# Expert slot weights made group by group, the gather placed behind the activation's transposes, and modulation vectors closed in four groups of 256 columns

## The chip, the cores and the metric

The kernel runs on one core of one Trainium2 chip. A core has a matrix engine (TensorE, "PE" in the profile, with its weight loads shown apart as "PEld"), a vector engine (VectorE, "DVE"), an engine for activation functions (ScalarE, "ACT"), a general engine (GpSimd, "POOL") and a queue that issues transfers (SyncE, "SP"). Every engine works through its own list of instructions in order; semaphores join them. Weights lie in the chip's main memory and come by DMA into the on-chip memory (SBUF, 128 partitions); products go into PSUM, of which this kernel uses eight banks of 128 x 512 fp32. The metric is the device time of one execution in microseconds. Before the change the median of three runs is 2223.85 us (2223.41 to 2227.16).

## The reference

One input of 256 tokens x 1024 goes through two stacks of two layers each, all in fp32. The first stack has, per layer, a feed-forward block, a mixing block of three kinds of attention, a cross attention over 256 memory rows, and a second feed-forward block. The second stack is driven by a vector `c`: six modulation vectors per layer are made from it, and each layer has a mixer and a layer of 32 experts. Cut to what the change touches:

```python
c_act = silu(c)
for l in range(2):
    mod = c_act @ w_ada[l] + b_ada[l]                       # 6 vectors of 1024
    shift_m, scale_m, gate_m, shift_f, scale_f, gate_f = split(mod, 6)
    h = rms_norm(x, norm_mix[l]) * (1 + scale_m) + shift_m
    x = x + gate_m * mixer(h)
    h = rms_norm(x, norm_ffn[l]) * (1 + scale_f) + shift_f
    # a token takes 1 of 4 expert groups, and 2 of its 8 experts, with weights comb[token, expert]
    for each expert e:
        y += (silu(h @ w_gate[e]) * (h @ w_up[e]) * comb[:, e]) @ w_down[e]
    x = x + gate_f * y
```

The reference computes every expert for every token, most of them with weight 0. The kernel computes each expert only for the tokens that chose it.

## The kernel before, in words

**Modulation vectors.** They are not needed before the second stack, and are made during the first one, in the feed-forward blocks. `ada_step` (line 1320) gives for each of the 12 vectors (2 layers x 6) and each quarter of the 1024 rows of `w_ada` a small function per piece. DVE multiplies the piece by `c_act` and adds it into a tile `ada` of 128 x 1024 (lines 1357, 1359), so that what is left is a sum over the 128 partitions. With the fourth quarter, `rows` asks SP for the bias row and, for two of the six vectors, the gain of the norm, each broadcast to 32 partitions per half of 512 columns (lines 1329, 1332). Then `close` is put into a list of small tasks that are worked in between the dense products. It sums over the partitions with a product against ones, one product per half of 512 columns, each into its own strip of 32 PSUM partitions (line 1339, tile `adap`); DVE adds the bias and applies the gain (1342, 1344) on the strips, and SP writes one row of each strip into a table in memory, `mods` (1347). The second stack reads the vectors from there. Each fp32 product shows as two records on PE.

Around it, the first stack multiplies in a split form: each weight piece of 512 columns is split by ACT and DVE into a high and a low part (lines 288 to 293) into one of eight slots, and PE makes three products of it for each of the two halves of the tokens (`mm3`, lines 303 to 305). Raw weights come in transfers of 1 MB into four buffers, which SP issues as the buffers are freed (line 280).

**Rounds of experts.** `moe` (line 1833) first finds the chosen experts and the rank of each token among the tokens of an expert; each expert has 32 slots (`CAP`). `one_round` then works in eight groups q of four experts, 128 slots in all. For a group:
- `places` (1939) makes the 0/1 matrices `P[t]` (128 tokens x slots, one per half of the tokens),
- `gather(q)` (1951) multiplies the normed input by `P`, in two PSUM banks of four pieces each, and ACT and DVE evict the pieces in turn, with scale and shift, into `xg` (1956 on ACT for even pieces, 1958 on DVE for odd ones); `xg` has two buffers,
- `gate_up(q, k)` for k = 0 to 7 (1964) takes a 1 MB chunk of gate and up weights; the four experts stand on four strips of 32 columns of PE (tile `gu`),
- ACT makes silu of the gate half (2003), DVE multiplies by the slot weight and the up half (2004),
- two transposes of the activation and two of `P` (2007, 2009), copied by DVE and ACT (2013, 2014),
- four chunks of down weights (2021, tile `dn`), split into high and low by ACT and DVE, and the product with the transposed `P` that adds the slots back to their tokens (2026, tile `ymoe`).

The slot weights are `comb`, per token, brought into the order of the slots by a product with `P`: today for all eight groups at once, at k = 7 of the first group (line 1987, tile `comb`, 16 products of 4 columns), then a product with a mask and a sum on DVE (1990, 1992) into `cs`, of which line 2004 takes one column per group.

Each layer has 96 chunks of 1 MB (64 of gate and up, 32 of down); they go into a ring of buffers in the order of use, and SP issues a load when its buffer's chunk has been used (lines 1726, and 1723 for chunks that are loaded in two halves).

**What sets the order.** Where the code stands under `manual_schedule`, PE, ACT, DVE and POOL keep the order in which it is written. That holds for the first stack, the mixer, and the first part of a round: the loop over k of group 0, with the block of the slot weights. The loop over q behind it does not stand there: a planner orders it, by what is ready in its own model of time and, among that, by what is written earlier. SP's order is the planner's everywhere. PSUM has six banks of one pool (`ymoe` takes four for the whole round, the gather's banks and `dn` share two) and two of another (`tp`: `gu`, the transposes, the slot weights). Line 2044 and what follows repeat the round where an expert has more than 32 tokens; in the profile each layer has one round.

## Time and profile before

| | |
|---|---|
| median of three runs | 2223.85 us |
| profiled execution | 2221.21 us, with a span of 2219.2 us |
| PE busy | 2108.2 us, 95% |
| DVE busy | 1350.9 us, 61% |
| ACT busy | 1157.7 us, 52% |
| moved by DMA | 552.96 MB, mean 249 GB/s |
| first round of experts | about 1652 to 1852 us |
| second round | about 2005 to 2208 us |

All times are microseconds from the span's start. A row of the order of time has the start, the length, the engine, the line, the operation, what it writes and reads, and in brackets how long the engine sat idle before it and what ended that. Rows of one kind that follow each other are merged ("x32"). PE's records are pipelined and their ends are modelled: what a record costs in a stream is read from start to start. SP's rows are issues of transfers, not the transfers. A wait is put down to what came last.

### The profile page before, as it was taken

Reading aid. Unit: us, or ns where it says so; the run is one execution under the profiler, and the core shown is the slowest. Engines: PE = TensorE matmul, PEld = TensorE weight load, DVE = VectorE, ACT = ScalarE, POOL = GpSimd, SP = SyncE. Lnnn points to the kernel's source line nnn. Section 1 sums busy time; section 2 is a strip of 40 time slices with the busy share of each in tenths; the row PEclk is TensorE's granted clock in tenths of the full one; section 3 lists DMA queues with packets and bytes.
Section 4 is the critical chain, followed back from the end, with each engine's and each line's share of the span. In section 5 each row is a group of like instructions: output and inputs, shape, how many; then the busy total and the mean of one; then the engine's idle time right before and its main releaser. Section 6 shows DMA issues by size and latency. Waiting matters only on the chain. (4 is left out here: it accounts for less than half of the span.)

```text
span 2219.2 us, 28887 instructions
## 1 busy us (share of the span) xinstructions
PE 2108.2 (95%) x10668; PEld 1561.2 (70%) x10668; DVE 1350.9 (61%) x2472; ACT 1157.7 (52%) x2196; POOL 68.4 (3%) x76
## 2 busy tenths in 40 slices
PE   8999999999999999999999999998999887998895
PEld 7887878888788788777788878876765333775341
DVE  6876767765787687676677558766562114563111
ACT  6555677565655555466766556545842112762110
POOL 0000000000000000000000000002000001100000
PEclk9999999999999999999999999999999898999998
DMA  7875534553687577744356437766489998569998
GB/s 290 315 246 203 191 117 168 192 194 128 218 286 240 201 277 260 261 169 152 133 182 225 152 126 276 261 248 242 152 315 380 418 418 331 220 240 370 418 417 338
DMA packets 94551, 552.96 MB, mean 249 GB/s; under 512 B 11223, under 2 KB 12954, under 8 KB 41398
## 3 DMA queue, kind: packets, MB, share of 16 engines
q1 hardware_dynamic: 94398, 550.99, 67.0%
q8 instruction: 88, 1.44, 0.3%
q14 instruction: 65, 0.53, 0.1%
HBM read 549.85 MB, written 1.10 MB: 248 GB/s over the span
## 5 line engine op out<-in xcount | busy, mean ns | idle before, releaser
L289 DVE SCALAR_TENSOR_TENSOR hl<-raw,g_pre,hl 128x512 fp32r<-128x512 f32 (+1 forms) x296 | 214.2, 744 | 46.1 <-ACT hl L288 45.6
L288 ACT ACTIVATE hl<-raw,g_pre 128x512 fp32r<-128x512 f32 (+1 forms) x296 | 204.5, 719 | 62.4 <-PE gu L305 24.9
L289 DVE SCALAR_TENSOR_TENSOR pair<-raw,g_pre,pair 128x512 fp32r<-128x512 f32 (+1 forms) x296 | 207.6, 744 | 46.1 <-ACT pair L288 43.5
L293 DVE TENSOR_TENSOR hl<-raw,hl 128x512 fp32r<-128x512 f32 (+1 forms) x286 | 192.7, 688 | 68.8 <-ACT hl L291 65.5
L288 ACT ACTIVATE pair<-raw,g_pre 128x512 fp32r<-128x512 f32 (+1 forms) x296 | 196.6, 715 | 71.8 <-PE gu L305 52.0
L291 ACT ACTIVATE hl<-raw 128x512 fp32r<-128x512 f32 (+1 forms) x290 | 176.9, 626 | 94.3 <-PE y L305 41.1
L1964 PE MATMUL gu<-raw,xg 128*32 128x512 f32 x1024 | 144.0, 633 | 25.2 <-DMA raw<-w_gu 23.0
L293 DVE TENSOR_TENSOR pair<-raw,pair 128x512 fp32r<-128x512 f32 (+1 forms) x184 | 119.8, 692 | 69.7 <-ACT pair L291 69.3
L291 ACT ACTIVATE pair<-raw 128x512 fp32r<-128x512 f32 (+1 forms) x188 | 107.4, 621 | 91.6 <-PE y L305 64.3
L303 PE MATMUL gu<-pair,hh 128*128 128x512 f32 x320 | 127.3, 398 | 0.0
L303 PE MATMUL gu<-hl,hh 128*128 128x512 f32 x320 | 126.3, 395 | 0.0
L305 PE MATMUL gu<-pair,hl 128*128 128x512 f32 x320 | 125.1, 391 | 0.0
L305 PE MATMUL gu<-hl 128*128 128x512 f32 x320 | 125.0, 391 | 0.0
L304 PE MATMUL gu<-pair,hh 128*128 128x512 f32 x320 | 124.8, 390 | 0.0
L304 PE MATMUL gu<-hl,hh 128*128 128x512 f32 x320 | 124.8, 390 | 0.0
L1359 DVE SCALAR_TENSOR_TENSOR ada<-raw,cact,ada 128x512 f32<-128x512 f32 x168 | 122.0, 745 | 0.0
L1964 PEld LDWEIGHTS gu<-raw,xg 128*32 128x32 f32 x1024 | 29.8, 112 | 107.2 <-DMA raw<-w_gu 52.9
L1951 PEld LDWEIGHTS gather<-P,u 128*128 128x128 f32 x512 | 69.0, 214 | 30.3 <-issue 21.3
L2021 PE MATMUL dn<-raw,aT 128*32 128x512 f32 x512 | 79.2, 623 | 10.2 <-DMA raw<-w_dn 3.0
L2004 DVE SCALAR_TENSOR_TENSOR sil<-sil,cs,gu 128x256 f32<-128x256 f32 x16 | 7.7, 481 | 124.0 <-ACT sil L2003 123.7
L298 DVE TENSOR_TENSOR y<-dn,y 128x512 fp32r<-128x512 f32 x32 | 22.1, 692 | 98.5 <-ACT y L297 98.4
L1956 ACT ACTIVATE xg<-gather,fm 128x128 f32<-128x128 f32 x64 | 29.2, 457 | 95.4 <-PE gather L1951 80.6
(672 smaller groups left out, 4879.3 us busy)
## 6 DMA issues: line engine op xcount, KB each, us to landing
raw<-w SPq DMA_DIRECT2D x131, 1024.0 KB
raw<-w_gu SPq DMA_DIRECT2D x98, 1024.0 KB
raw<-win SPq DMA_DIRECT2D x71, 1024.0 KB
raw<-w_dn SPq DMA_DIRECT2D x54, 1024.0 KB
raw<-w_ada SPq DMA_DIRECT2D x48, 1024.0 KB
raw<-w_gu SPq DMA_DIRECT2D x60, 512.0 KB
raw<-w_out SPq DMA_DIRECT2D x16, 1024.0 KB
raw<-cross_wkv SPq DMA_DIRECT2D x16, 1024.0 KB
```

The lines of the kernel that those rows point to most:

```text
L288: nc.scalar.activation(hi, raw[:, c0:c0 + n], AF.Copy, scale=gain)
L289: nc.vector.scalar_tensor_tensor(lo, raw[:, c0:c0 + n], gain, hi.bitcast(F32), op0=ALU.mult, op1=ALU.subtract)
L291: nc.scalar.activation(hi, raw[:, c0:c0 + n], AF.Copy)
L293: eng.tensor_tensor(out=lo, in0=raw[:, c0:c0 + n], in1=hi.bitcast(F32), op=ALU.subtract)
L303: te.matmul(out, xh, wh, start=start, stop=False)
L304: te.matmul(out, xh, wl, start=False, stop=False)
L305: te.matmul(out, xl, wh, start=False, stop=stop)
L1359: nc.vector.scalar_tensor_tensor(self.ada[:, c], w, act, self.ada[:, c], op0=ALU.mult, op1=ALU.add)
L1951: te.matmul(ps[:, (k - k0) * 128:(k - k0 + 1) * 128], hm[t][:, k * 128:(k + 1) * 128], P[t][:, q * 128:(q + 1) * 128], start=(t == 0), sto ...
L1956: nc.scalar.activation(xg[:, k, :], v, AF.Identity, bias=sh, scale=g)
L1964: te.matmul(gu[32 * e:32 * e + 32, :], xg[:, k, 32 * e:32 * e + 32], w(e), start=(k == 0), stop=(k == 7))
L2021: te.matmul(dn[half][32 * e:32 * e + 32, :], aT[:, f, 32 * e:32 * e + 32], w(e), start=(f == 0), stop=(f == 1))
```

## The change

The change has two parts.

In `ada_step`, a vector is closed in four groups of 256 columns in place of two of 512: four products of 256 columns on four strips of 32 partitions, bias and gain broadcast in four pieces, DVE's operations on 128 x 256 in place of 64 x 512, and four rows written to `mods`.

In `one_round`, the slot weights of a group are made in the group itself, by two products of 4 columns into a tile of their own, with a product and a sum on DVE, written between the group's gate and up products and its activation. The block for all groups at once is gone. The gather of the next group is written behind the group's transposes and their copies, where it stood ahead of the activation. In the first gather of a round, piece k = 1 is evicted by ACT and not by DVE.

```diff
-            for g in range(2):
-                p, c0 = slice(32 * g, 32 * g + 32), g * 512
-                nc.sync.dma_start(bn[p, 0, :], self.a["b_ada"][l, i * D + c0:i * D + c0 + 512].unsqueeze(0)
-                                  .to_broadcast([32, 512]))
+            for g in range(4):
+                p, c0 = slice(32 * g, 32 * g + 32), g * 256
+                nc.sync.dma_start(bn[p, 0, 0:256], self.a["b_ada"][l, i * D + c0:i * D + c0 + 256].unsqueeze(0)
+                                  .to_broadcast([32, 256]))
                 if gain:
-                    nc.sync.dma_start(bn[p, 1, :], self.a[gain][l, c0:c0 + 512].unsqueeze(0).to_broadcast([32, 512]))
+                    nc.sync.dma_start(bn[p, 1, 0:256], self.a[gain][l, c0:c0 + 256].unsqueeze(0).to_broadcast([32, 256]))
...
-            for g in range(2):
-                nc.tensor.matmul(tp[32 * g:32 * g + 32, :], self.ones[:, 0:32], acc[:, g * 512:(g + 1) * 512],
+            for g in range(4):
+                nc.tensor.matmul(tp[32 * g:32 * g + 32, 0:256], self.ones[:, 0:32], acc[:, g * 256:(g + 1) * 256],
                                  start=True, stop=True)
-            row = fp.tile([64, 512], F32, tag="row", name="row")
-            nc.vector.tensor_add(row, tp[0:64, :], bn[0:64, 0, :])
+            row = fp.tile([128, 256], F32, tag="row", name="row")
+            nc.vector.tensor_add(row, tp[:, 0:256], bn[:, 0, 0:256])
             if gain:
-                nc.vector.scalar_tensor_tensor(row, row, 1.0, bn[0:64, 1, :], op0=ALU.add, op1=ALU.mult)
-            for g in range(2):
-                c0 = i * D + g * 512
-                nc.sync.dma_start(self.mod_dram[l:l + 1, c0:c0 + 512], row[32 * g:32 * g + 1, :])
+                nc.vector.scalar_tensor_tensor(row, row, 1.0, bn[:, 1, 0:256], op0=ALU.add, op1=ALU.mult)
+            for g in range(4):
+                c0 = i * D + g * 256
+                nc.sync.dma_start(self.mod_dram[l:l + 1, c0:c0 + 256], row[32 * g:32 * g + 1, :])
...
-                            if k % 2 == 0:
+                            if k % 2 == 0 or (first and k == 1):
                                 nc.scalar.activation(xg[:, k, :], v, AF.Identity, bias=sh, scale=g)
...
-                    xg = gather(0, {0: ((0, 1), (1, 2)), 1: ((2, 4),), 3: ((4, 8),)}[0])
+                    xg = gather(0, {0: ((0, 1), (1, 2)), 1: ((2, 4),), 3: ((4, 8),)}[0], first=True)
...
-                        if k == 7:
-                            comb_tp = self.tp("comb")
-                            for i in range(8):
-                                for t in range(2):
-                                    te.matmul(comb_tp[:, i * 4:(i + 1) * 4], P[t][:, i * 128:(i + 1) * 128],
-                                              comb[:, t, i * 4:(i + 1) * 4], start=(t == 0), stop=(t == 1))
-                            cw, cs = r2.tile([128, 8, 4], F32, name="cw"), r2.tile([128, 8], F32, name="cs")
-                            ve.tensor_mul(cw, comb_tp[:, 0:32].rearrange("p (q e) -> p q e", q=8),
-                                          self.misc[:, 34:38].unsqueeze(1).to_broadcast([128, 8, 4]))
-                            ve.reduce_sum(cs, cw, AX.X)
...
-                    if q < 7:
-                        xg = gather(q + 1)
+                    ctp, cw, cs = self.tp("comb"), r2.tile([128, 4], F32, name="cw"), r2.tile([128, 1], F32, name="cs")
+                    for t in range(2):
+                        te.matmul(ctp[:, 0:4], P[t][:, q * 128:(q + 1) * 128], comb[:, t, q * 4:(q + 1) * 4],
+                                  start=(t == 0), stop=(t == 1))
+                    ve.tensor_mul(cw, ctp[:, 0:4], self.misc[:, 34:38])
+                    ve.reduce_sum(cs, cw, AX.X)
...
-                    ve.scalar_tensor_tensor(sil, sil, cs[:, q:q + 1], gu[:, 256:512], op0=ALU.mult, op1=ALU.mult)
+                    ve.scalar_tensor_tensor(sil, sil, cs, gu[:, 256:512], op0=ALU.mult, op1=ALU.mult)
...
                     nc.scalar.activation(PT, tp[:, 256:512].rearrange("p (f s) -> p f s", f=2), AF.Copy)
+                    if q < 7:
+                        xg = gather(q + 1)
```

More of the change, by code (lines that the diff above doesn't have):

```diff
@@ L1942, in places, with gather @@
                                          op=ALU.is_equal)
-                def gather(q, cuts=((0, 4), (4, 8)), xg=None):
+                def gather(q, cuts=((0, 4), (4, 8)), xg=None, first=False):
                     if xg is None:
```

## The prediction

> **What bounds the kernel now.** I read the page first, then busy time by stage, then the order of time at the two places that the diff touches.
>
> ```profile
> span 2219.2 us, 28887 instructions
> PE 2108.2 (95%) x10668; PEld 1561.2 (70%) x10668; DVE 1350.9 (61%) x2472; ACT 1157.7 (52%) x2196; POOL 68.4 (3%) x76
> 30.00:1500.00 1470.00, 1455.96 (x6819) 1178.76 (x6818) 1062.83 (x1899) 876.59 (x1689) 27.44 (x40) 1.00 0.60 210
> 1692.00:1852.00 160.00, 136.97 (x869) 56.04 (x867) 26.17 (x53) 25.11 (x53) 0.00 (x0) 0.90 1.02 418
> 2045.00:2208.00 163.00, 133.53 (x861) 51.89 (x860) 26.49 (x54) 24.07 (x51) 0.00 (x0) 0.94 1.00 412
> ```
>
> The columns of the stretches are length, busy PE, PEld, DVE, ACT, POOL, granted clock, DMA share and GB/s. There are two regimes. In the first stack (to about 1500 us), where the modulation vectors are made, PE has work for all but 14 us of 1470 (clock 1.00), while DMA's share is 0.60. In the expert rounds (1652 to 1852 and 2005 to 2208) PE has gaps and DMA runs at share 1.00 to 1.02, some 412 to 418 GB/s. So an edit in the first stack is worth what it takes off PE's queue, and an edit in a round is worth only what it takes out of the DMA's idle time.
>
> **The closings of the modulation vectors.** One closing, PE's order of time (start, length, line):
>
> ```profile
> 75.16 0.39 PE L305 MATMUL gu<-hl 128*128 128x512 f32 x1
> 75.47 1.05 PE L1339 MATMUL adap<-ada,ones 128*32 128x512 f32 x4
> 76.46 0.50 PE L303 MATMUL gu<-pair,hh 128*128 128x512 f32 x1
> 1686.12 1.07 PE L1964 MATMUL gu<-raw,xg 128*32 128x512 f32 x8
> 1687.12 0.74 PE L2026 MATMUL ymoe<-y,PT 128*128 128x512 f32 x2
> 1971.08 1.07 PE go L1651 x24
> ```
>
> The closing's 4 records (two products of 512 columns, two records each) hold PE from 75.47 to 76.46, 0.99 us. The row of 1686.12 is one expert chunk: 8 records, four products of 512 columns on four column strips, from 1686.12 to 1687.12, 1.00 us. Twice the products in the same time: strips run side by side, and the time goes by columns. Five chunks back to back take 4.43 us (1662.21 to 1666.64, quoted below); with a lone one at 1.00 the other four take 0.86 each, so 0.14 of a lone chunk is its end draining. The four products of 256 columns are then 0.86/2 + 0.14 = 0.57 us, a gain of 0.43 us. Bounds: if each record had a slot of its own in PE's queue of the size that a chunk's 8 records show (0.86/8), 8 short records would take as long as before, a gain of 0. Against that stands the last row: 24 records of small products in 1.07 us, 0.045 us each, so 8 need only 0.36, less than the 0.43 of streaming. I take 0.43. There are 12 closings:
>
> ```profile
> L1339 PE MATMUL adap<-ada,ones x48: 592/604/618, 75.5 to 1493.4; 128*32 128x512 f32 x48
> L1342 DVE TENSOR_TENSOR row<-adap,bn x12: 671/681/684, 78.1 to 1494.0; 64x512 f32<-64x512 f32 x12
> L2013 DVE COPY aT<-actT 128x256 f32<-128x256 f32 x8 | 3.4, 421 | 4.2 <-PE actT L2009 4.2
> L1329 SPq DMA_DIRECT2D bn<-b_ada x24: 413/423/610, 62.3 to 1441.6; - x24
> L1332 SPq DMA_DIRECT2D bn<-n_mix x4: 413/427/733, 108.8 to 859.0; - x4
> L1332 SPq DMA_DIRECT2D bn<-n_ffn x4: 413/417/423, 662.5 to 1414.2; - x4
> L1347 SPq DMA_DIRECT2D mods<-row x24: 236/244/292, 78.8 to 1495.0; - x24
> ACT hl L288 <- DMA raw<-w: 21.9, 13, 3.4
> ACT pair L291 <- PE y L305: 64.3, 35, 3.3
> ```
>
> 48 records are 12 closings of 4, all between 75.5 and 1493.4 us, where PE is full: 12 x 0.43 = **5.2 us** (0 to 5.2). On DVE each row operation shrinks from 0.681 toward that of 128x256 elements (0.421 by the copy from PSUM), some 0.26 us; 12 of them and 4 of L1344 are about 4 us of DVE time, costed at nothing because PE's queue is what is full (DVE 1063 of 1470). SP gets dearer: L1329 and L1332 together go from 32 to 64 issues of about 0.42 us, L1347 from 24 to 48 of 0.244, so 32 x 0.42 + 24 x 0.244 = 19.3 us more of SP's time, 0.84 or 1.68 us ahead of a closing and 0.49 behind it. Weight loads queue behind these on SP, the splits (ACT L288/L291, DVE L289/L293) wait for the loads, and PE for the splits. I cost it at nothing: the splits more often stand waiting for PE to give a slot back (64.3 us in the one row, more in its fellows) than for a load (21.9 us in the other), so they run ahead by the slots there are, and a load that is 1 or 2 us late meets finished splits. Without that cover it is up to 19.3 us. The row also reaches the write to memory earlier, by 0.43 + 0.26 us, so SP stands less long at L1347.
>
> **The start of a round.** The first round's chain, then the second's:
>
> ```profile
> 1653.32 0.46 ACT L1956 ACTIVATE xg<-gather,fm 128x128 f32<-128x128 f32 x1 [4.73 <-PE gather L1951]
> 1653.79 1.28 ACT L1891 ACT_TABLE_LOAD   x1
> 1654.17 0.41 DVE L1958 TENSOR_SCALAR xg<-gather,fm 128x128 f32<-128x128 f32 x1 [2.03 <-PE gather L1951]
> 1654.50 2.50 DVE L1939 TENSOR_TENSOR P<-rank,misc 128x128 f32<-128x128 f32 x8
> 1659.24 1.06 PE L1964 MATMUL gu<-raw,xg 128*32 128x512 f32 x8 [0.73 <-ACT xg L1956]
> 1662.21 4.50 PE L1964 MATMUL gu<-raw,xg 128*32 128x512 f32 x40
> 1666.64 3.73 PE L1987 MATMUL comb<-comb,P 128*128 128x4 f32 x32
> 1670.24 5.45 PE L1951 MATMUL gather<-P,u 128*128 128x128 f32 x32
> 1677.02 0.63 PE L2021 MATMUL dn<-raw,aT 128*32 128x512 f32 x3
> ```
>
> ```profile
> 2012.54 1.07 PE L1964 MATMUL gu<-raw,xg 128*32 128x512 f32 x8 [1.52 <-ACT xg L1956]
> 2019.95 3.73 PE L1987 MATMUL comb<-comb,P 128*128 128x4 f32 x32
> 2023.54 3.82 PE L1951 MATMUL gather<-P,u 128*128 128x128 f32 x32
> 2028.70 0.63 PE L2021 MATMUL dn<-raw,aT 128*32 128x512 f32 x3
> ```
>
> Moving k = 1 of the first gather to ACT lets DVE begin the eight P pieces 1.9 us sooner: it now waits 2.03 us for the gather (1654.17) and only then goes on. ACT does 0.46 us more. Behind the P pieces DVE runs the weights' chain, whose second exponential stands on ACT ahead of the k = 2 eviction, for which PE waits at 1659.24 (0.73 us) and 2012.54 (1.52 us). ACT's table load for the exponential now comes behind the k = 1 eviction, so the chain gains about 1.2 us, not 1.9: PE gains **0.73 us** in the first round and **1.2** in the second (bounds 0 and the whole waits).
>
> **The slot weights.** Now 32 records of 4 columns stand between the last chunk of group 0 and the gather of group 1: 1666.64 to 1670.24, 3.60 us (3.59 in the second round), 0.1125 us a record. Behind them come the gather, the transposes and the first down products at 1677.02 and 2028.70. The change leaves 4 records there (0.45 us) and moves 28 to the other seven groups, one set of 4 in each: **3.15 us** leave this place in each round. The gather behind the transposes costs PE nothing of its own: it is ready while ACT and DVE make the activation, so I expect the planner to fill PE with gather records until the transposes are ready, and to put the rest behind them. From the end of group 0 to the first down product are now 10.4 us, in the second round 8.75, of which 3.59 are the sets, 3.82 the gather (5.45 in the first round) and the rest the transposes and the copy behind them. Without 3.15 of them they are 7.2 and 5.6; where the copy lies under gather records it is up to 1 us less. I use the 3.15, plus the start's 0.73 and 1.2: a shift of at least 3.9 and 4.3 us.
>
> What is late next? The moved sets cost 7 x 0.45 = 3.15 us of PE in groups 1 to 7, and two small DVE operations each; from 1692 and 2045 on DMA sets the pace and PE has gaps (137 of 160 us busy), so this lies in the gaps. Each new tile of the two-buffer PSUM pool is free again after the small DVE product, ahead of the transposes' tile, so the chunks of the next group don't wait for it.
>
> **What the shift is worth.** SP's issues and the DMA there:
>
> ```profile
> 1664.17 3.64 SPq L1723 DMA_DIRECT2D raw<-w_gu  x6
> 1678.89 6.64 SPq L1726 DMA_DIRECT2D raw<-w_gu  x5
> ```
>
> ```profile
> SPq L1726 <- PE dn L2021: 24.3, 6, 11.0
> ```
>
> ```profile
> 1676.00:1680.00 4.00, 4.00 (x36) 1.53 (x34) 1.15 (x3) 1.15 (x4) 0.00 (x0) 1.00 0.16 39
> 1680.00:1684.00 4.00, 4.00 (x20) 1.17 (x22) 0.69 (x1) 0.35 (x1) 0.00 (x0) 1.00 0.93 356
> 2028.00:2032.00 4.00, 4.00 (x34) 1.37 (x26) 1.05 (x3) 1.29 (x3) 0.00 (x0) 1.00 0.57 170
> 2032.00:2036.00 4.00, 4.00 (x23) 1.29 (x25) 0.69 (x1) 0.03 (x1) 0.00 (x0) 1.00 0.90 369
> ```
>
> From 1667.8 to 1678.89 SP issues nothing; it waits for the first down product to free a buffer (11.0 us, the longest). The transfers issued until then are over at about 1676, and DMA drops to 39 GB/s. Against 420 GB/s the two slices lose 4 x (381 + 64)/420 = 4.2 us in the first round, and 4 x (250 + 51)/420 = 2.9 us in the second. Shortfalls ahead of them I leave. The five loads behind the first hole are spread over 6.64 us, so the later ones wait for PE too; a shift of 3.9 us doesn't quite close a hole of 4.2: between 3.2 (the 3.15 alone) and 4.2 I take **3.7**. The second closes: **2.9**. Both are 0 if the issue doesn't move. Behind the holes DMA is full to the round's end, so its end, and all that follows, moves by this.
>
> One price works against spreading the sets. A chunk that is followed by work on the whole array takes 1.00 in place of 0.86 us, 0.14 for draining; with as much on the way back (an estimate) a set among chunks costs 0.45 + 0.28 = 0.73 us, seven of them 5.1 in place of 3.15. [...]
>
> **Sum.** 5.2 + 3.7 + 2.9 = 11.8 us less. The profiled execution took 2221.21 us, 2.0 around its span of 2219.2; it becomes 2209.4 with a span of 2207.4. The median of the runs, 2223.85, lies 2.6 above the profiled one; on it the forecast is **2212.0 us**.
>
> **The rivals.**
> *The closings gain nothing* (records are paced one by one, or the splits pace PE): -6.6, 2217.2. For it: DVE, whose splits feed PE, is the next fullest engine. Against: PE without a gap there, and the 0.045 us records.
> *The holes stay.* The planner's order is not written in the code; it may put group 1's chunks, or the whole gather with its evictions, ahead of the first down product, and the buffer that SP waits for comes as late as now. Only the closings count: -5.2, 2218.7. Against: the 3.15 us leave PE's queue whatever the order.
> *PE paces the rounds*, and each set pays both switches: per round 5.1 - 3.15 = 2.0 more less the start's 0.73 or 1.2, about +2 in all, so -5.2 + 2 = -3.2, 2220.7. For it: PE is full in the slices of the holes (4.00 of 4.00). Against: behind them DMA is full for 160 us while PE is not.
> *Slower: SP's queue.* The 32 broadcast issues and 24 writes stand in one queue with the weight loads. If loads become late by all of it, the closings' -5.2 turns into +14.1, and with the holes closed the sum is +7.5: 2231. It decides once 11.8 of the 19.3 us reach PE, that is where splits have under about 1 us of lead at most closings. For it: ACT waits 3.4 us for one load at worst. Against: 21.9 us of such waits in 13 places over 1500 us.
>
> **How the numbers follow.** Forecast 0.55; closings worthless 0.10; holes stay 0.17; PE paces 0.07; SP's queue 0.08; the last 0.03 for more than forecast: 4.2 in place of 3.7, the whole of the waits at the rounds' starts (0.73 + 1.52) and the slow gather of the first round mended (5.45 - 3.82 = 1.6) would be 4.4 more, 2207.6. The range from 2206 to 2222 holds all but the SP case and the tail of the others. No change can be told from 0.2%, 4.4 us: faster is below 2219.4, same to 2228.3. Faster: forecast, closings worthless, the better tail, and a little over half of the holes case, 0.78; same 0.14; slower 0.08.
>
> **What would show it.** Right: closings of 8 records that hold PE some 0.57 us; PE still without gaps before 1500; 4 comb records and not 32 behind group 0; SP's silence after the sixth half-load shorter by 4 us or more; no 4-us slice under 0.9 of DMA between there and the round's end; rounds shorter by 3.7 and 2.9 us, the mixing stage of the second layer unchanged. Wrong: PE gaps or ACT waits on weight loads around the closings; the first down product still 8 us behind group 0; DMA holes that only moved to a later group.

## The result, and the profile after

The changed kernel takes **2210.87 us** (median of 4 runs, 2210.41 to 2211.02), beside 2224.26 us (2223.41 to 2227.16, 4 runs) for the kernel before: ratio 0.9935, 95% interval 0.992 to 0.9951, 13.4 us less: a small gain, clear of the noise. The forecast was 2212.0. The profiled execution took 2211.02 us for a span of 2209.2; before they were 2221.21 and 2219.2, so between the two profiled executions there are only 10.2 us. Where the other 3 lie is part of what follows.

First the head of the page of the changed kernel, and busy time by the stretches that the prediction read (length, busy PE, PEld, DVE, ACT, POOL, granted clock, which is the share of full speed that PE was given, DMA share, GB/s):

```profile
span 2209.2 us, 29059 instructions
PE 2102.9 (95%) x10716; PEld 1559.4 (71%) x10716; DVE 1351.7 (61%) x2498; ACT 1159.1 (52%) x2198; POOL 68.3 (3%) x76
30.00:1500.00 1470.00, 1455.91 (x6886) 1181.98 (x6885) 1061.27 (x1903) 878.75 (x1694) 28.07 (x41) 1.00 0.60 210
1687.00:1847.00 160.00, 135.00 (x863) 54.23 (x855) 28.66 (x65) 22.98 (x48) 0.00 (x0) 0.91 1.02 417
2037.00:2198.00 161.00, 135.52 (x864) 53.00 (x860) 26.69 (x62) 22.14 (x48) 0.00 (x0) 0.90 1.00 412
```

The two regimes are as they were: PE is full to 1500 us (14 us of gaps in 1470, as before), and DMA is full in the rounds behind their first groups (1.02 and 1.00). The change did not alter what bounds a stage.

**A closing.** PE's order of time around the first closing of the changed kernel, then its groups and waits:

```profile
74.83 0.64 PE L1339 MATMUL adap<-ada,ones 128*32 128x256 f32 x8
75.40 0.50 PE L303 MATMUL gu<-pair,hh 128*128 128x512 f32 x1
...
L1339 PE MATMUL adap<-ada,ones x96: 379/391/403, 74.8 to 1488.0; 128*32 128x256 f32 x96
L1342 DVE TENSOR_TENSOR row<-adap,bn x12: 415/424/426, 77.4 to 1488.4; 128x256 f32<-128x256 f32 x12
L1329 SPq DMA_DIRECT2D bn<-b_ada x48: 320/420/1050, 61.6 to 1437.4; - x48
ACT hl L288 <- DMA raw<-w: 17.2, 9, 3.5
```

From 74.83 to 75.40 the 8 records hold PE for 0.57 us, where 4 held it for 0.99. SP's broadcasts doubled in number at the same 0.42 us each, and the row of ACT's waits for weight loads that the prediction read did not grow: 17.2 us in 9 places, before 21.9 in 13.

**Behind group 0 of the first round.** PE's order of time in the changed kernel, then what SP issued, its wait for the down products around the first round (1640 to 1700), and the 4-us slices there:

```profile
1660.65 0.61 PE L1992 MATMUL comb<-comb,P 128*128 128x4 f32 x4
1661.11 2.70 PE L1951 MATMUL gather<-P,u 128*128 128x128 f32 x22
1663.65 0.38 PE L2001 MATMUL actT<-ident,sil 128*128 128x128 f32 x2
1663.87 0.38 PE L2003 MATMUL actT<-ident,P 128*128 128x128 f32 x2
1664.09 1.28 PE L1951 MATMUL gather<-P,u 128*128 128x128 f32 x10
1665.30 1.92 PE L2017 MATMUL dn<-raw,aT 128*32 128x512 f32 x16
```

```profile
1658.17 3.39 SPq L1723 DMA_DIRECT2D raw<-w_gu  x6
1666.42 7.03 SPq L1726 DMA_DIRECT2D raw<-w_gu  x5
...
SPq L1726 <- PE dn L2017: 19.2, 8, 6.4
...
1660.00:1664.00 4.00, 4.00 (x38) 3.36 (x31) 1.12 (x4) 0.84 (x2) 0.00 (x0) 1.00 0.93 346
1664.00:1668.00 4.00, 4.00 (x32) 1.82 (x30) 1.73 (x6) 2.36 (x5) 0.00 (x0) 1.00 0.98 376
1668.00:1672.00 4.00, 4.00 (x23) 1.28 (x25) 0.61 (x1) 0.00 (x0) 0.00 (x0) 1.00 1.04 421
```

The planner filled PE as the prediction expected: one set of 4 slot-weight records, 22 gather records while ACT and DVE make the activation, the transposes, the last 10 gather records while DVE copies. The first down product stands 4.65 us behind the end of group 0 (1665.30 less 1660.65); before it was 10.38 (1677.02 less 1666.64). SP's silence behind the sixth half-load is 4.9 us (1661.56 to 1666.42) in place of 11.1, 6.2 shorter where 4 or more was forecast; in the second round it is 4.5 in place of 9.7. SP's longest wait for a down product in the first round is 6.4 us in place of 11.0, and the sum of these waits there 19.2 in place of 24.3. The slice of 39 GB/s is gone; the lowest share is 0.93, and from 1668 to the round's last issue no slice of 4 us is under 0.99. In the second round the lowest is 0.98, from 2012 to 2016.

**A ledger of the whole.** Two marks divide the time behind the first stack: the first product of the ranks (L1879, once a round) and SP's last issue of a down weight in each round. Each kernel was profiled twice (the second time as an experiment, below). The rank products, and the last issue of the first and the second round, of the kernel before; of its second profile; of the changed kernel; of its second profile:

```profile
L1879 PE MATMUL rank<-selb,beforeb x2: 206/207/208, 1651.0 to 2004.3; 128*128 128x32 bf16 x2
1842.80 0.33 SPq L1726 DMA_DIRECT2D raw<-w_dn  x1
2195.75 0.33 SPq L1726 DMA_DIRECT2D raw<-w_dn  x1
```

```profile
L1879 PE MATMUL rank<-selb,beforeb x2: 209/210/210, 1651.4 to 2007.2; 128*128 128x32 bf16 x2
1845.75 0.33 SPq L1726 DMA_DIRECT2D raw<-w_dn  x1
2197.57 0.33 SPq L1726 DMA_DIRECT2D raw<-w_dn  x1
```

```profile
L1879 PE MATMUL rank<-selb,beforeb x2: 206/206/207, 1645.8 to 1996.6; 128*128 128x32 bf16 x2
1834.49 0.33 SPq L1726 DMA_DIRECT2D raw<-w_dn  x1
2184.89 0.33 SPq L1726 DMA_DIRECT2D raw<-w_dn  x1
```

```profile
L1879 PE MATMUL rank<-selb,beforeb x2: 206/206/207, 1646.1 to 1997.8; 128*128 128x32 bf16 x2
1835.47 0.33 SPq L1726 DMA_DIRECT2D raw<-w_dn  x1
2185.87 0.33 SPq L1726 DMA_DIRECT2D raw<-w_dn  x1
```

| stretch | before, its second profile | changed, its second profile | difference of the means | predicted |
|---|---|---|---|---|
| start to first rank | 1651.0, 1651.4 | 1645.8, 1646.1 | -5.25 | -5.2 |
| first rank to last issue | 191.8, 194.35 | 188.7, 189.4 | -4.0 | -3.7 |
| to second rank (mixing stage) | 161.5, 161.45 | 162.1, 162.3 | +0.7 | 0 |
| second rank to last issue | 191.45, 190.4 | 188.3, 188.1 | -2.7 | -2.9 |
| to the end of the span | 23.45, 25.3 | 24.3, 23.5 | -0.5 | 0 |
| span | 2219.2, 2222.9 | 2209.2, 2209.4 | -11.75 | -11.8 |

Four profiles are few. Over all fourteen of this case the first rank starts at 1650.8 to 1652.2 us in the eight whose closings use two strips, and at 1645.8 to 1646.9 in the six with four, 5.0 less in the mean.

### The profile page after: what moved, and what is told of

The parts are those of the page before. It is cut to its first block, busy times and chain, and to the rows that moved or that the text cites. A ratio compares the mean times of both kernels' runs of the same rounds, so it can differ in the third digit from the quotient of the medians.

```text
span 2209.2 us, 29059 instructions
## 1 busy us (share of the span) xinstructions
PE 2102.9 (95%) x10716; PEld 1559.4 (71%) x10716; DVE 1351.7 (61%) x2498; ACT 1159.1 (52%) x2198; POOL 68.3 (3%) x76
## 3 DMA queue, kind: packets, MB, share of 16 engines
q8 instruction: 87, 1.43, 0.3%
## 5 line engine op out<-in xcount | busy, mean ns | idle before, releaser
L293 DVE TENSOR_TENSOR hl<-raw,hl 128x512 fp32r<-128x512 f32 (+1 forms) x286 | 191.8, 685 | 69.7 <-ACT hl L291 66.5
L1951 PE MATMUL gather<-P,u 128*128 128x128 f32 x512 | 76.0, 302 | 5.2 <-DVE xg L1958 3.8
L1997 ACT ACTIVATE sil<-gu 128x256 f32<-128x256 f32 x16 | 6.1, 384 | 137.0 <-PE gu L1964 137.0
```

The costliest lines, as they stand in the source:

```text
L293: eng.tensor_tensor(out=lo, in0=raw[:, c0:c0 + n], in1=hi.bitcast(F32), op=ALU.subtract)
L1951: te.matmul(ps[:, (k - k0) * 128:(k - k0 + 1) * 128], hm[t][:, k * 128:(k + 1) * 128], P[t][:, q * 128:(q + 1) * 128], start=(t == 0), sto ...
```

## The experiments

Each time stands beside runs of the kernel before on the same chip; a difference is one of medians, and brackets hold the 95% interval of the ratio.

### The two parts by themselves

closings_only is the kernel before with the changed rows() and close(). rounds_only is the changed kernel with these two put back. Of the two edits only the heads of the loops are shown:

```diff
 closings_only                      rounds_only
-for g in range(2):  # 512 columns  -for g in range(4):  # 256 columns
+for g in range(4):  # 256 columns  +for g in range(2):  # 512 columns
```

> The kernel before with the four-group closing alone. Theory A (PE paces the first stack and a closing costs its streamed columns): 12 x 0.43 = 5.2 us less, all of it before 1500 us, the two rounds as before, so that the rank products of the first and the second round both start 5.2 us sooner (1645.8, 1999.1) and the span is 2214.0. Rival B (a gain there is used up later, since the rounds wait for transfers): less than 3 us at the end. Rival C (the closing gains only together with the round's change): 0.

> The kernel before with the three edits of the expert rounds and the old closing. Theory A (the two parts add up): the rank products of the first round start as before (1651.0), those of the second 2.5 us sooner, the end 4.8 us sooner, span 2214.4. Rival B (the earlier end of the first stack changed what the rounds gain): the rounds' gain lies 1 us or more off 4.8.

Beside 2224.16 us: closings_only 2217.49 (2216.78 to 2218.74), ratio 0.9967 [0.9954, 0.9979], 6.7 less; rounds_only 2217.41 (2217.03 to 2217.67), 0.9963 [0.9949, 0.9977], 6.75 less. Together 13.4, all that the change gives: in the medians the parts add up. By the marks, the first rank starts at 1646.6 in closings_only and at 1651.1 in rounds_only, and the rounds are 192.1 and 190.6 us in the first, 187.8 and 188.4 in the second. So each part acts in its own stage. "The closings gain nothing" and "the holes stay" both fall.

The sizes do not fit as well as the sum. The first rank of closings_only is 4.4 us sooner than in the first profile of the kernel before, where 5.2 was expected, and its median gains 6.7; what the other 2 us are isn't shown. The rounds of rounds_only are 7.0 us shorter than in that profile, where 4.8 was expected. Both have a longer tail than it, 25.3 and 26.1 us in place of 23.45, so that their spans, 2216.3 and 2215.6, lie above the 2214.0 and 2214.4 that were expected.

### How a closing gets shorter

two_strips is the kernel before, with the same two strips of the array and the same row, but 4 products of 256 columns (8 records) in place of 2 of 512. broadcasts_x3 is the changed kernel with every broadcast of a bias or gain issued three times. Arguments left out are marked by dots:

```diff
 two_strips
-            for g in range(2):
-                matmul(tp[32 * g:32 * g + 32, :], ..., acc[:, g * 512:(g + 1) * 512], ...)
+            for h in range(2):
+                for g in range(2):
+                    c0 = g * 512 + h * 256
+                    matmul(tp[32 * g:32 * g + 32, h * 256:(h + 1) * 256], ..., acc[:, c0:c0 + 256], ...)
 broadcasts_x3
+                for _ in range(3):
                     nc.sync.dma_start(bn[p, 0, 0:256], ...)
                     if gain:
                         nc.sync.dma_start(bn[p, 1, 0:256], ...)
```

> The kernel before with each closing as four products of 256 columns, but on the two old strips, two products one behind the other on each: the same records as in the change (8 per closing), without the four strips. Transfers and DVE's operations as before. Theory A (strips run side by side, time goes by the columns of one strip): a closing holds PE 0.99 us as before, span 2219.2 within 1 us. Rival B (shorter products are cheaper by themselves): 0.57 us a closing, 5 us less. Rival C (records are paced one by one): 1.2 us a closing or more, 2 us longer.

> The changed kernel with each broadcast of a bias or gain row issued three times into the same place: 128 more issues on SP, some 54 us of its time in all, 3.4 or 6.7 us ahead of a closing. Theory A (splits run ahead of PE by up to eight slots, so late loads meet finished splits): under 1.5 us longer. Rival B (SP's queue is on the path once it is late by more than some 2 us): 10 us or more longer, with ACT waiting for weight loads around the closings.

Beside 2224.41 us: two_strips 2223.9 (2218.7 to 2232.06), 0.9999 [0.9987, 1.001]; broadcasts_x3 2210.38 (2209.77 to 2211.16), 0.9931 [0.9915, 0.9948]. The first closing on PE in two_strips:

```profile
75.90 1.06 PE L1341 MATMUL adap<-ada,ones 128*32 128x256 f32 x8
76.89 0.50 PE L303 MATMUL gu<-pair,hh 128*128 128x512 f32 x1
```

0.99 us, as long as 4 records of 512 columns on the same two strips. So it is not the shorter product that pays, nor does twice the number of records cost: with the same columns per strip the closing stays as long, with half of them it shrinks to 0.57. The span of two_strips is 2221.2 where 2219.2 within 1 us was expected; its tail, 25.4 us in place of 23.45, makes that up. SP's queue is no cost either: 128 more issues of 0.42 us, 54 us of SP's time, leave the time where it was. ACT's waits for weight loads are 17.7 us in the row shown above, and 26.8 over its three rows (19.5 over two in the changed kernel), so some of the delay reaches ACT, and none that could be told reaches the end. The slower rival, which rested on 19.3 us of SP, falls.

### The three edits of a round, one at a time

weights_only makes the slot weights group by group, with the gather at its old place; gather_only moves the gather alone; first_only puts k = 1 of the first gather on ACT alone. All else is as in the kernel before.

```diff
 weights_only
+                    ctp, cw, cs = ...   # one set of 4 records a group, in place of 32 behind group 0
 gather_only
-                    if q < 7:           # ahead of the activation
-                        xg = gather(q + 1)
...
+                    if q < 7:           # behind the transposes and their copies
+                        xg = gather(q + 1)
 first_only
-                            if k % 2 == 0:
+                            if k % 2 == 0 or (first and k == 1):
```

> The slot weights made group by group, with the gather of the next group still written ahead of the activation and k = 1 of the first gather on DVE. Theory A (what counts is that 28 records, 3.15 us, leave PE's queue between group 0 and the first down product): nearly the whole gain of the rounds, 3.5 to 4.8 us, first down product 5.6 us behind group 0 in the second round, silence of SP ahead of it 3 us shorter. Rival B (the place of the gather is what frees the buffer sooner): under 2 us.

> The gather of the next group written behind the transposes and their copies, with the block of slot weights left as it was and k = 1 on DVE. Theory A (the 3.15 us of slot weights are the gain): between 0 and 1.5 us, first down product still 7.5 us or more behind group 0. Rival B (the gather's place is the gain): 3 us or more, since the activation and the transposes come out 3.8 us sooner.

> Only the eviction of k = 1 of the first gather goes from DVE to ACT. Theory A (PE's waits of 0.73 and 1.52 us for the k = 2 piece go, but DMA's hole behind group 0 only shrinks by as much): 0.7 us in the first round and 1.2 in the second, about 2 us in all. Rival B (the hole is set by the down product's other waits): 0 to 0.5 us.

| kernel | median (range) | before beside it | ratio | first down product behind group 0 | rounds, rank to last issue |
|---|---|---|---|---|---|
| weights_only | 2218.55 (2217.12 to 2220.79) | 2224.16 | 0.9971 [0.9961, 0.9981] | 6.32, 6.32 | 189.2, 189.3 |
| gather_only | 2221.11 (2217.64 to 2224.59) | 2224.16 | 0.9987 [0.9977, 0.9997] | 9.40, 9.41 | 190.0, 190.4 |
| first_only | 2222.62 (2220.97 to 2223.54) | 2224.41 | 0.9988 [0.9978, 0.9998] | 10.37, 8.74 | 191.6, 191.2 |
| rounds_only (all three) | 2217.41 (2217.03 to 2217.67) | 2224.16 | 0.9963 [0.9949, 0.9977] | 4.66, 4.64 | 187.8, 188.4 |

Alone they give 5.6, 3.05 and 1.8 us, together 6.75 and not 10.5, but each of these medians can be off by some 2 us by its interval. By the marks, against the first profile of the kernel before, the rounds are 4.7, 2.8 and 0.4 us shorter, 7.9 in all beside 7.0 for the three together, so the overlap is smaller than the medians make it. weights_only has its first down product 6.32 us behind group 0 and not the 5.6 expected, because its set stands between the gather and the transposes. What overlap there is has a reason: in weights_only DMA already moves 408 GB/s or more, at a share of 1.00 or more, in every slice of 4 us from 20 us behind the rank on, and no more can be had there by an earlier down product. What rounds_only has beyond it, 1.4 and 0.9 us, would have to lie ahead of that: in the slice from 12 to 16 us behind the rank weights_only moves 293 and 299 GB/s, rounds_only 393 and 395. In gather_only the first chunk's down products run without others between them, so that SP's issue behind its silence comes 26.2 us behind the rank in place of 27.9 in the first round, and 26.1 in place of 26.3 in the second; the round is 1.8 and 1.0 us shorter. The first of these fits, the second is more than the issue explains and stays open. So gather_only reaches the 3 us of rival B, but not for B's reason: its transposes start 7.5 us behind group 0 in both rounds, where they started 8.9 and 7.25 before, and not 3.8 sooner, since PE takes 20 of the 32 gather records ahead of them all the same. In first_only SP's issue comes 0.8 and 0.3 us sooner behind the rank, but the rounds are only 0.2 and 0.3 us shorter, and its 1.8 us are hardly clear of nothing.

### What the spread sets cost

no_slot_weights is the changed kernel without the sets of 4 records and their two small DVE operations; the activation is multiplied by a column of constants, so the slot weights are left out.

```diff
-                    ctp, cw, cs = ...
-                    for t in range(2):
-                        te.matmul(ctp[:, 0:4], P[t]..., comb[:, t, q * 4:(q + 1) * 4], ...)
-                    ve.tensor_mul(cw, ctp[:, 0:4], self.misc[:, 34:38])
-                    ve.reduce_sum(cs, cw, AX.X)
+                    cs = self.misc[:, 34:35]
```

> The changed kernel without the slot weights: the products with P, the mask product and the sum are left out, and a constant column stands in their place, so the experts' outputs are not weighted. It takes 16 products of 4 columns and 16 DVE operations out of each round. Theory A (the spread sets lie in PE's gaps, only the set behind group 0 is on the path, and DMA has no hole left there): within 0.8 us of the changed kernel's 2209.2 span. Rival B (PE paces the rounds and each set pays two switches of mode): 16 x 0.73 = 11.7 us less, or at least 3 us less.

2210.7 us (2209.03 to 2212.56), 0.9935 [0.9918, 0.9952], the same ratio as the changed kernel's; rounds of 188.4 and 187.8 us, 0.3 and 0.5 below its first profile. The first down product comes 0.45 us sooner. The span, 2207.2, is 2.0 below the changed kernel's and so outside the 0.8 of theory A, but the rest of it stands in the mixing stage and the tail, where there are no sets, and the median shows none of it. So the sets among the chunks cost no more than the scatter, and with them the two switches a set, ahead of it and behind it, that the prediction estimated at 0.28 us a set and 2.0 us a round: "PE paces the rounds" falls. PE's rows of the changed kernel show most of that price. At 1737.01, 2088.14 and 2171.99 us a set stands between two chunks: the chunk ahead of it takes 0.99 or 1.00 us from start to start in place of 0.86, and the set 0.54 us up to the next chunk, where it takes 0.46 or 0.47 up to a gather. That is 0.68 us a set among chunks, beside the 0.73 estimated. The closing's 0.57 us are what 0.43 of columns and the 0.14 by which a lone chunk is longer add up to; that these 0.14 are a drain, as the prediction calls them, no run shows. But among chunks DMA sets the pace (shares of 1.02 and 1.00), and the 0.68 us there cost nothing that these runs can tell.

### What the clock does

The kernel before scatters over 4 to 11 us (4 to 21 runs), the changed one over 0.6 (4 runs), and the two first profiles account for 10.2 of 13.4 us. Both kernels were profiled again, and two more built: wide_block is the kernel before with its 32 products of 4 columns made 128 columns wide (the slot weights are left out by that); warm_tail is the changed kernel with each of the last chunks multiplied a second time into a bank that nothing reads.

```diff
 wide_block
-                                    te.matmul(comb_tp[:, i * 4:(i + 1) * 4], P[t]..., comb[:, t, i * 4:(i + 1) * 4], ...)
+                                    te.matmul(comb_tp[:, i % 4 * 128:(i % 4 + 1) * 128], P[t]..., hm[t][:, i * 128:(i + 1) * 128], ...)
 warm_tail
                     for e in range(4):
                         te.matmul(gu[32 * e:32 * e + 32, :], xg[:, k, ...], w(e), ...)
+                    if pre is None and ahead and q == 7 and k >= 2:
+                        warm = self.tp("comb")
+                        for e in range(4):
+                            te.matmul(warm[32 * e:32 * e + 32, :], xg[:, k, ...], w(e), start=True, stop=True)
 # and the same behind the first three down chunks of q == 7
```

> The kernel before, profiled a second time. In its first profile the ranks of the two rounds start at 1651.0 and 2004.3 us, the two rounds take 191.8 and 191.45 us up to the last issue of a down weight, and 23.45 us are left behind that issue; most other runs leave 24 to 26 there. Theory 1 (the first profile had a lucky tail): the two starts and the two rounds again within 0.7 us, the tail 24.5 to 26, span 2220.5 to 2222. Theory 2 (the kernel before varies in its rounds, by the clock behind the block of small products): the tail within 0.5 us of 23.45 and a round longer or shorter by over 1 us. Theory 3 (it varies in the first stack): the first rank moved by over 1 us.

> The changed kernel, profiled a second time. First profile: ranks at 1645.8 and 1996.6, rounds of 188.7 and 188.3 us up to the last issue, 24.3 us behind it, clock 1.00 in the slices behind group 0 of both rounds. Expected again within 0.7 us, the clock 1.00 there. If the clock behind group 0 is 0.6 in this one, the clock there is chance and not the block's doing.

> The kernel before, but the 32 products of 4 columns behind group 0 become 32 products of 128 columns with the same weights, in the same place (their values are of no use, so the slot weights are left out of the result). 32 gather records of 128 columns take 3.8 us at clock 1.00, so the block stays about as long as its 3.7 us. Theory 1 (blocks of 4-column products make the clock drop): clock 1.00 and not 0.6 in the slice behind the block of the first round, the gather there 3.8 us in place of 5.45, the first down product 8.7 us behind group 0 in place of 10.4, the first round 190.2 to 190.8 us in place of 191.8; in all about 1.3 us less than before. Theory 2 (the clock drops there for another reason, such as the start of the round or the idle stretch ahead of it): clock 0.6 and a gather of 5.4 us again, the round 191.8, no change.

> The changed kernel with idle work on TensorE in the last group of the second round of the second layer: from the third chunk on, and behind the first three down chunks, the four products of the chunk once more, into a bank that nothing reads. Theory 1 (the end of the kernel goes by the granted clock, which falls where TensorE waits for each chunk): clock 1.00 behind the last issue of a down weight, the 16 records of the first down products 2.1 to 2.3 us in place of 3.25, the closing ones no longer 1.9 to 3; the end 23.4 us or less behind the last issue in place of 24.3; in all 0.9 us less than the changed kernel's profile. Theory 2 (the extra chunks stand ahead of the transposes and of the closing products, and delay them by as much as they save): the end 24.3 to 25.5 us behind the last issue, and a time within 0.5 us of the changed kernel's or above it.

Beside 2225.2 us (2222.2 to 2233.19, 17 runs): before_again 2224.92 and after_again 2211.14 (one run each), wide_block 2221.93 (2219.99 to 2224.01), 0.998 [0.9968, 0.9992], warm_tail 2215.29 (2211.88 to 2216.12), 0.9943 [0.9924, 0.9962]. The block behind group 0, the gather behind it and the slices of 4 us at the gather's start and, in the first of the two, at DMA's hole behind it (18 GB/s), in the second profile of the kernel before, then in wide_block:

```profile
1667.06 4.79 PE L1987 MATMUL comb<-comb,P 128*128 128x4 f32 x32
1671.72 6.01 PE L1951 MATMUL gather<-P,u 128*128 128x128 f32 x32
...
1670.00:1674.00 4.00, 4.00 (x20) 4.00 (x21) 0.86 (x3) 0.00 (x0) 0.00 (x0) 0.50 1.01 399
1678.00:1682.00 4.00, 4.00 (x36) 1.52 (x34) 1.15 (x3) 1.15 (x4) 0.00 (x0) 1.00 0.11 18
```

```profile
1666.45 3.84 PE L1987 MATMUL comb<-u,P 128*128 128x128 f32 x32
1670.12 3.74 PE L1951 MATMUL gather<-P,u 128*128 128x128 f32 x32
...
1670.00:1674.00 4.00, 4.00 (x38) 4.00 (x37) 1.68 (x5) 1.02 (x3) 0.00 (x0) 1.00 1.01 412
```

In before_again the clock is 0.50 behind the block, the block takes 4.79 us in place of 3.73 and the gather 6.01 in place of 5.45, the first down product stands 12.0 us behind group 0 in place of 10.38, and the round is 194.35 us in place of 191.8. That is the round of theory 2 of its expectation beside the longer tail of theory 1 (25.3 us): the kernel before varies in both places, and neither theory holds whole. With 128 columns the block lasts as long, and the clock is 1.00, the gather 3.74, the down product 8.74 behind group 0, the round 190.7 us: by this one profile it is the few columns that the low clock follows, and not the place of the block or the time that it takes (the values that are multiplied are others too). In median the wide block is 3.3 us below the kernel before, of which the marks explain 1.1 beside its first profile and 3.6 beside its second.

after_again repeats after to 0.7 us, but for a second rank 1.2 later and a tail 0.8 shorter, with a clock of 1.00 behind group 0 of both rounds. The last group on PE, in the first profile of the changed kernel, in its second, and in warm_tail:

```profile
2174.91 1.06 PE L1964 MATMUL gu<-raw,xg 128*32 128x512 f32 x8 [1.31 <-DMA raw<-w_gu]
2177.40 1.78 PE L1964 MATMUL gu<-raw,xg 128*32 128x512 f32 x8 [1.43 <-DMA raw<-w_gu]
...
2184.87 1.94 PE L1964 MATMUL gu<-raw,xg 128*32 128x512 f32 x8 [0.56 <-DMA raw<-w_gu]
...
2191.96 3.25 PE L2017 MATMUL dn<-raw,aT 128*32 128x512 f32 x16 [0.52 <-DVE aT L2007]
```

```profile
2188.35 1.54 PE L1964 MATMUL gu<-raw,xg 128*32 128x512 f32 x8 [0.57 <-DMA raw<-w_gu]
...
2192.09 2.43 PE L2017 MATMUL dn<-raw,aT 128*32 128x512 f32 x16 [0.52 <-DVE aT L2007]
```

```profile
2188.20 1.07 PE L1964 MATMUL gu<-raw,xg 128*32 128x512 f32 x8 [0.58 <-DMA raw<-w_gu]
2189.09 1.04 PE L1969 MATMUL comb<-raw,xg 128*32 128x512 f32 x8
2190.22 0.61 PE L1996 MATMUL comb<-comb,P 128*128 128x4 f32 x4
2191.85 0.44 PE L2005 MATMUL actT<-ident,sil 128*128 128x128 f32 x2 [1.03 <-DVE sil L2002]
```

The extra chunks do hold the clock in this stage: a chunk takes 1.07 us in place of 1.93. And they lose: each stands in PE's queue ahead of what the kernel waits for (the slot weights behind the last chunk, the closing products behind the down chunks), the clock falls all the same, to 0.50 and 0.68 in the two slices from 2193.72 to 2197.72, and the tail becomes 27.5 us in place of 24.3. That is theory 2 with a larger price than expected: 4.4 us above the changed kernel's median.

## Why the prediction was right, step by step

**The closings: 5.2 forecast, 5.25 measured by the four profiles, 5.0 by all fourteen.** The working held in each term: 0.57 us on PE in place of 0.99, 12 times, at a place where PE has no gap; the row operation 0.424 us (0.421 from the copy); SP's extra 19.3 us without effect. The lower bound, a slot of 0.86/8 us for each record in PE's queue, is refuted by the changed closing itself, whose 8 records take 0.57 us; the 0.99 of two_strips would have fitted it.

**The first hole: 3.7 forecast; 3.1 between the first profiles, 5.0 between the second, 4.0 in the mean. The second hole: 2.9 forecast; 3.15 and 2.3, 2.7 in the mean.** The mechanism is the one named: down product sooner, buffer free sooner, SP's issue sooner, DMA without a hole, and a round that ends sooner by the hole. Sizes inside the chain were off and did not show in the sum. The down product moved by 5.7 us (4.1 in the second round) behind group 0, not by the 3.15 used: the copy did come to lie under gather records (up to 1 us, named and left out), and the gather of the first round fell from 5.45 us to its normal length, which the prediction had put into its last rival at 3 in 100. What exceeds the hole buys nothing: SP's issue behind its silence came 7.3 and 5.3 us sooner behind the rank, and the rounds ended 3.1 and 3.2 us sooner (first profiles). The cap by the hole, 4.2 and 2.9 us read from two slices each, is why the sum held. The shift was larger than the 3.9 and 4.3 us of the prediction; that this does not show in the sum is owed to the cap.

**The start of a round: 0.73 and 1.2 us were forecast** for k = 1 on ACT. From the rank to the end of group 0 there were 15.64 and 15.65 us, 15.66 and 15.60 in the second profile; now 14.85 and 15.19, and 15.40 and 15.33: 0.25 to 0.8 us. This is the step that failed most. PE runs there at a clock of 0.50 in the 4 us behind the rank, and with k = 1 on ACT the length goes by the clock of the next 4 us: 15.4 us where it was 0.58, 14.85 at 0.73, 14.48 at 0.98 (rounds_only), which is near the forecast. With k = 1 on DVE it stays at 15.6 to 15.7 at any clock from 0.62 to 1.00. It cost the forecast little, since weights_only closes the hole without it.

**Outside the sum.** The mixing stage was to stay unchanged: 161.4 to 162.6 us over all kernels, the changed one at the upper half, +0.7; no order of kernels explains it. The tail goes with the first 16 down records of the last group, and so with the clock there: 23.4 to 23.5 us where these take 2.1 to 3.1 us, 24.3 at 3.25 and 3.32, 25.3 to 26.1 at 3.64 (all profiles but warm_tail's).

**The step from the profile to the median** was wrong. The prediction set the 2.6 us, by which the median lies above the profiled execution of the kernel before, on top of its forecast for the profile. The changed kernel doesn't have them: its profiled executions (2211.02, 2211.14) are its median (2210.87). So the sum, 11.8, was 1.6 too large for the first pair of profiles, the offset was 2.6 too large for the median, and the forecast came out 1.1 too high. That it came so close is in part luck: the two errors have opposite signs. before_again shows what an offset can be made of: a first round of 2.5 us more and a tail of 1.9 more. Of the 2.5 us, 1.6 are the longer block and gather at the lower clock, which the change does away with.

**The rivals** fell one by one, as told. Of the terms of "PE paces the rounds" the 0.14 us for the way back was the author's estimate; no run shows it, and PE's rows have 0.08 there (0.54 less 0.46). The last one (more gain) was right that the slow gather of the first round would go and wrong that this would add to the gain.

## What to carry to other kernels

Where products use one strip of the array in four, ask whether the same columns can be cut over more strips: here PE was held by the columns of the fullest strip and not by the number of records (0.99 us with 4 records and with 8 of the same columns per strip, 0.57 with half the columns). In a stage that DMA bounds, look for the slice in which DMA is not full, follow back which buffer the next issue waits for, and take work out from between; what was taken beyond the hole's length was worth nothing here, and what was put elsewhere in the same stage cost nothing that could be told. Before a median is forecast from one profile, profile the kernel before a second time: here a single one lay 3 us from its own median.

## What the runs showed of the hardware that was not expected

**Products of few columns were followed by a lower clock while the records show PE busy.** In all six profiles of kernels with the block of 32 products of 4 columns, the clock of the first round is 0.50 to 0.65 in a slice of 4 us that begins some 4 us behind the block's start; PE's busy time there is 4.00 of 4.00. In the eight profiles without the block it is 1.00. In the second round, with the same block, only one of the six shows it (gather_only, 0.64); why the others escape isn't settled. Nor is it shown what about the products of 4 columns the clock follows: the ends of the records are modelled, and the only other width that was tried, 128 columns in wide_block, stays at 1.00 in its one profile.

**The clock fell and came back while PE waited a little for each chunk.** In the last group a chunk comes each 2.5 us. At 1.00 it takes 1.06 us and PE waits some 1.4; behind waits of 1.31 and 1.43 us in the changed kernel the chunks take 1.93 us at 0.50, and PE waits 0.55 to 0.71. It stays so for the rest of the chunks and into the first down products, 3.25 us. In the second profile the clock comes back during the last chunk, with the same waits of 0.57 us, and the down products take 2.43. So the short waits don't keep the clock low by themselves. In warm_tail, with two chunks' work in each 2.5 us and waits of 0.57, the chunks stay at 1.00. No wait of the last group ahead of the fall is longer than 1.43 us in the changed kernel's first profile. Which way an execution goes made 0.8 us of tail in the two profiles of the changed kernel and 1.9 in those of the kernel before, and no run here controls it without paying more.

**The scatter of the kernel before** (2221 to 2233 us over all chips) shrank to 0.6 us, in four runs on one chip. Its first round and its tail vary with the clock, by the two profiles. That the block makes the scatter isn't shown: weights_only (3.7 us), wide_block (4) and no_slot_weights (3.5) scatter without it, and closings_only (2.0) and first_only (2.6) scatter little with it.
